# Hybrid mixer layer: scan branch rebuilt by chunks of four state tiles, its elementwise work and the gate sums from GpSimd to VectorE

## The chip, the cores and the metric

One core of a Trainium2 chip runs the whole program. The metric is the device time of one execution in microseconds (us). A run has several executions; of the kernel before three were timed, and one more was executed with the profiler.

## The reference, cut to what matters

Two layers, one after the other, on a sequence of 256 positions with 2048 features. A layer normalizes its input, projects it with one wide matrix, feeds four branches a to d of width 512 with slices of the projection, and sums them under gates:

```python
def _layer(x, ...):
    h = _rmsnorm(x, norm_g)
    proj = h @ w_in
    ya, yb, yc = ...                        # two attentions and a matrix recurrence
    yd = _branch_s5(d_u, ...) * silu(d_z)
    up = einsum('bsnw,nwd->bsnd', stack([ya, yb, yc, yd]), w_up)
    gates = sigmoid(gate + merge_b)
    merged = sum(gates * up, over the four branches)
    return x + merged @ w_out

def _branch_s5(u, ...):                     # 32 groups, 16 inputs and 64 complex states each
    bu_re, bu_im = einsum(u, bb_re), einsum(u, bb_im)
    x = scan over time of  x[t] = a * x[t-1] + bu[t]        # a complex
    y = einsum(x_re, c_re) - einsum(x_im, c_im) + d_skip * u
    y = gelu(y);  return y * sigmoid(y @ glu_w + glu_b)
```

The change concerns the branch d (`_branch_s5`) from the product with `bb` to the sum with `d_skip * u`, and the sum over the four branches.

## The kernel before, in words

**Weights and blocks.** Nearly all the work of TensorE is products of 128 positions (two halves t) with weight blocks of 512 columns. Weights come from HBM by SP's queue in units of 512 KB (tile `raw`, 1024 columns on 128 partitions). ScalarE rounds a unit to `wh` and VectorE computes `wl = raw - wh` (class `Stream`, line 355, `split`, line 369, three units ahead of their use). `block` (line 432) then makes three matmuls for each 128 rows and half: `wh*hH`, `wl*hH`, `wh*hL`. A projection block has 16 x 2 x 3 = 96 matmuls, an up block (a branch's output with `w_up`) 24. The two halves of a block go into two of four PSUM banks with the name `mm`, so a block can start once the block before the last has been evacuated.

**Order.** `layer_sequence` lists the blocks of a layer: first the projections for the branches, from the dilated attention on with gate blocks and up blocks in between, then the remaining gate and up blocks with `glu` behind the thirteenth gate, then the blocks with `w_out`. Work of the branches is written as generators (chains e, q, m, b, c, a, d; d is the scan branch). After each weight unit `tick` (line 411) steps these chains in the order `eqmbcad`, as long as a planner (class `Plan`, line 135) believes that VectorE, ScalarE and GpSimd are at most 2600 ns ahead of TensorE (`free`, line 202) and that what the step yielded as its needs is ready with two of four banks free (`can`, line 194). The planner holds a price for each instruction (class `Eng`, line 207) and assumes that VectorE and GpSimd shut each other out where they share a port (`port`, line 151). Each engine works through its instructions in the order in which they are issued. Since all go through one helper, every row has line 253, and instructions are told apart by their tiles.

**The scan branch** (`d_scan`, line 1207). The 2048 complex states lie in 16 tiles of 128, four to a chunk c. The rotation of the states is taken out by cosine and sine tables of a chunk (`d_table`, line 1143: its second step is eight instructions on VectorE, `dk` and `dr`, one pair for each tile), which leaves a real scan. For a tile: `enter` (line 1219) makes the input products (`dbu`, for two tiles together, 12 matmuls of 32 rows, each tile on its own row strip of the array), multiplies them by cosine and sine on VectorE (from PSUM into `dm`), and GpSimd adds and subtracts them. `scan` (line 1240) runs two `tensor_tensor_scan` on VectorE, then two products with cosine and sine on GpSimd (`dm`, `dn`). `leave` (line 1250) subtracts and adds on VectorE. The loop is a pipeline: step i enters tile i, scans tile i-1 and leaves tile i-2. After every second tile the output products (`dyp`) of two tiles follow, 32 output columns each on its own column strip, and one VectorE instruction per pair adds `d_skip * u` into `uT`. One step of the next chunk's table is taken behind each tile's scans, in the same step of the chain.

**The sum over branches** (`merge`, line 1379). Behind an up block VectorE multiplies its two PSUM banks by the gate, and for all but the first branch GpSimd adds the 1024 columns into the sum (`gate<-gate`, 12 per layer).

**Other users of GpSimd** that stay there: the small instructions of the reciprocal roots (`rsqrt`, line 461; for the attention's queries and keys in `a_evac`, line 694, whose PSUM banks are freed only by the product `aqk<-mm,ass` on VectorE behind the root), and the phases of the tables.

Of the kernel before, what the change touches and what calls it, by code (L numbers as in the profile page):

```python
# [12 lines left out]
ALU = mybir.AluOpType  # L13
AX = mybir.AxisListType

P = 128
S = 256
# [241 lines left out]
def hybrid_kernel(ctx: ExitStack, tc: tile.TileContext, x_in, pos, win, wup, wout, wuq, wukv, wglu, pp_in, db_in,  # L259
# [3 lines left out]
    V, A = Eng(plan, "DVE", nc.vector), Eng(plan, "ACT", nc.scalar)  # L263
    T, G = Eng(plan, "PE", nc.tensor), Eng(plan, "POOL", nc.gpsimd)
# [28 lines left out]
    def h2(shape, dt=F32, name="h2"):  # L293
        return hp.tile(shape, dt, tag="h2", name=name)
# [8 lines left out]
    def brps(name="br"):  # L303
        t = pbr.tile([P, 512], F32, tag="br", name=name)
        plan.bank(t)
        return t
# [171 lines left out]
    def bc(ap, shape):  # L478
        return ap.to_broadcast(shape)
# [663 lines left out]
    def d_table(o, c):  # L1143

        iota = c_("iota")
        r, k = s4([P, 4, S], name="dr"), s4([P, 4, S], name="dk")
        for j in range(4):
            i = 4 * c + j
            V.tensor_scalar(k[:, j], iota, o.dfull[:, i:i + 1], MAGIC, op0=ALU.mult, op1=ALU.add)
        V.tensor_scalar(k, k, MAGIC, None, op0=ALU.subtract)  # L1150
        yield
        for j in range(4):
            i = 4 * c + j
            V.scalar_tensor_tensor(k[:, j], iota, o.dhi[:, i:i + 1], k[:, j], op0=ALU.mult, op1=ALU.subtract)
            V.scalar_tensor_tensor(r[:, j], iota, o.dlo[:, i:i + 1], k[:, j], op0=ALU.mult, op1=ALU.add)
        yield
        cosT = s4([P, 4, S], name="cosT")
        yield from half_angle(r, r, cosT, k, cosT)
        o.tab[c] = (cosT, r)
        yield  # L1160
# [46 lines left out]
    def d_scan(o):  # L1207
        yield (o.du,)
        uT = s4([P, 4, S], name="uT")
        to_T(o.du, uT)  # L1210
        uH, uL = s4([P, 4, S], F32R, name="uH"), s4([P, 4, S], F32R, name="uL")
        A.copy(uH, uT)
        V.tensor_tensor(uL, uT, uH.bitcast(F32), op=ALU.subtract)
        o.tab = {}
        yield from d_table(o, 0)
        yield (uH, uL, o.bbH, o.bbL)
        xs, bu = {}, {}

        def enter(i):
            c, j = divmod(i, 4)  # L1220
            if i % 2 == 0:
                for i2 in (i, i + 1):
                    bu[i2] = brps("dbu").rearrange("p (r s) -> p r s", r=2)
                for r in range(2):
                    for i2 in (i, i + 1):
                        q = slice(32 * (i2 % 4), 32 * (i2 % 4) + 32)
                        for n, (w, u) in enumerate(((o.bbH, uH), (o.bbH, uL), (o.bbL, uH))):
                            T.matmul(bu[i2][:, r], lhsT=w[q, r, c], rhs=u[q, c], start=(n == 0), stop=(n == 2),
                                     tile_position=(32 * (i2 % 4), 0))
            ps = bu.pop(i)  # L1230
            cs = bc(o.tab[c][0][:, j][:, None, :], [P, 2, S])
            sn = bc(o.tab[c][1][:, j][:, None, :], [P, 2, S])
            m1, m2 = h2([P, 2, S], name="dm1"), h2([P, 2, S], name="dm2")
            V.tensor_tensor(m1, ps, cs, op=ALU.mult)
            V.tensor_tensor(m2, ps, sn, op=ALU.mult)
            G.tensor_tensor(m1[:, 0], m1[:, 0], m2[:, 1], op=ALU.add)
            G.tensor_tensor(m1[:, 1], m1[:, 1], m2[:, 0], op=ALU.subtract)
            xs[i] = (m1, m2, cs, sn)

        def scan(i):  # L1240
            m1, m2, cs, sn = xs[i]
            mg = bc(o.mag[:, i:i + 1], [P, S])
            for r in range(2):
                V.tensor_tensor_scan(m2[:, r], mg, m1[:, r], 0.0, op0=ALU.mult, op1=ALU.add)
            n2 = h2([P, 2, S], name="dn2")
            G.tensor_tensor(m1, m2, cs, op=ALU.mult)
            G.tensor_tensor(n2, m2, sn, op=ALU.mult)
            xs[i] = (m1, n2)

        def leave(i):  # L1250
            x, n2 = xs[i]
            V.tensor_tensor(x[:, 0], x[:, 0], n2[:, 1], op=ALU.subtract)
            V.tensor_tensor(x[:, 1], x[:, 1], n2[:, 0], op=ALU.add)
            xs[i] = x

        nxt = iter(())
        for i in range(19):
            if i < 16:
                c = i // 4
                if i % 4 == 0:  # L1260
                    if c:
                        for _ in nxt:
                            yield
                    nxt = d_table(o, c + 1) if c < 3 else iter(())
                enter(i)
                yield (xs[i - 1][0],) if i else ()
            if 0 <= i - 1 < 16:
                scan(i - 1)
                next(nxt, None)
                yield xs[i - 2] if i > 1 else ()  # L1270
            if i >= 2 and i - 2 < 16:
                leave(i - 2)
                c, j = divmod(i - 2, 4)
                if j % 2:
                    yield (xs[i - 3], xs[i - 2])
                    yp = brps("dyp")[:, :S]
                    for jj in (j - 1, j):
                        q = slice(32 * jj, 32 * jj + 32)
                        x = xs.pop(4 * c + jj)
                        for r in range(2):  # L1280
                            T.matmul(yp[q, :], lhsT=o.dc[:, r, 4 * c + jj], rhs=x[:, r], start=(r == 0), stop=(r == 1),
                                     tile_position=(0, 32 * jj))
                    q = slice(32 * (j - 1), 32 * (j + 1))
                    V.scalar_tensor_tensor(uT[q, c], uT[q, c], o.p("dskip")[q, c:c + 1], yp[q],
                                           op0=ALU.mult, op1=ALU.add)
                yield (uH, uL)
        o.dyT = uT

    def d_gelu(o):
# [55 lines left out]
    o = new_layer(0)  # L1345
# [4 lines left out]
    ps = brps("warm")  # L1350
# [3 lines left out]
    for d in range(4):  # L1354
        xb = s4([P, 2, 512], name="xb")
        if d == 0:
            for i in range(2):
                q = slice(256 * i, 256 * i + 256)
# [11 lines left out]
    for l in range(depth):  # L1370
# [8 lines left out]
        def merge(nm, ps):  # L1379
            d, n = int(nm[1]), int(nm[2])  # L1380
            gt = gate_t.pop(nm)
            first = n == UP_ORDER[0]
            if first:
                acc_t[d] = gt
            acc = acc_t[d]
            for t in range(2):
                V.scalar_tensor_tensor(gt[:, t], gt[:, t], 1.0, ps[t], op0=ALU.add, op1=ALU.mult)
            if not first:
                G.tensor_tensor(acc, acc, gt, op=ALU.add)
            if n == UP_ORDER[-1]:  # L1390
                spawn("m", merged(o, d, acc_t.pop(d)))

# [13 lines left out]
        for kind, nm in layer_sequence(l):  # L1406
            if kind == "in":
                if nm[0] == "g":
                    d, n = int(nm[1]), int(nm[2])
# [3 lines left out]
                ps = proj(nm)  # L1413
# [32 lines left out]
                else:  # L1446
                    gt = s4([P, 2, 512], name="gate")
# [172 lines left out]
```

## Time and profile before

| | us |
|---|---|
| median of 3 executions | 2090.07 |
| lowest, highest | 2087.39, 2090.59 |
| the profiled execution, its own time | 2088.86 |
| its span, first to last instruction | 2086.7 |
| TensorE busy | 2065.0 |
| VectorE busy | 1418.9 |
| ScalarE busy | 1034.8 |
| GpSimd busy | 446.9 |

The profile is one execution recorded by the hardware. PE is TensorE's matmuls, PEld its weight loads, DVE is VectorE, ACT ScalarE, POOL GpSimd. A busy time counts the time in which at least one instruction of the engine runs. Matmuls are pipelined and their ends are modelled, so that the time between two starts says more than a duration. Float32 matmuls of the branches appear as two records each. PEclk is the granted clock of TensorE as a share of 2.4 GHz.

### The profile page before, as it was taken

Reading aid. Unit: us, or ns where it says so; the run is one execution under the profiler, and the core shown is the slowest. Engines: PE = TensorE matmul, PEld = TensorE weight load, DVE = VectorE, ACT = ScalarE, POOL = GpSimd, SP = SyncE. Lnnn points to the kernel's source line nnn. Section 1 sums busy time; section 2 is a strip of 40 time slices with the busy share of each in tenths; the row PEclk is TensorE's granted clock in tenths of the full one; section 3 lists DMA queues with packets and bytes.
Section 4 is the critical chain, followed back from the end, with each engine's and each line's share of the span. In section 5 each row is a group of like instructions: output and inputs, shape, how many; then the busy total and the mean of one; then the engine's idle time right before and its main releaser. Section 6 shows DMA issues by size and latency. Waiting matters only on the chain.

```text
span 2086.7 us, 26821 instructions
## 1 busy us (share of the span) xinstructions
PE 2065.0 (99%) x9764; PEld 1702.1 (82%) x9764; DVE 1418.9 (68%) x1817; ACT 1034.8 (50%) x1574; POOL 446.9 (21%) x702
## 2 busy tenths in 40 slices
PE   9999999999999999999999999999999999999999
PEld 7888887788888888888888888887777888888887
DVE  5566578778777766667556765858777667667664
ACT  6656464454544544444456564455554445444442
POOL 2533114321242000001043121323223300001010
PEclk9999999999999999999999999999999999999999
DMA  7554354445555556656655543455445555556564
GB/s 266 182 187 166 123 176 167 156 163 170 183 191 173 183 199 206 204 202 208 232 188 182 192 162 124 175 166 191 163 167 187 185 178 183 205 204 205 197 212 171
DMA packets 111012, 384.60 MB, mean 184 GB/s; under 512 B 12321, under 2 KB 13217, under 8 KB 110881
## 3 DMA queue, kind: packets, MB, share of 16 engines
q1 hardware_dynamic: 108576, 378.40, 53.2%
q10 hardware_dynamic: 2304, 4.50, 0.6%
q8 instruction: 76, 1.25, 0.2%
q14 instruction: 56, 0.45, 0.1%
HBM read 378.66 MB, written 4.19 MB: 183 GB/s over the span
## 4 chain that ended last, share of the span: by engine, by line
PE 95%; DVE 3%; DMA 1%; POOL 1%; ACT 0%; issue 0%; SPq 0%; DVEq 0%; ACTq 0%
PE mm L253 86%; PE mb L253 2%; PE pv L253 1%; DVE dk L253 1%; PE tt L253 1%; PE dyp L253 1%; PE sc L253 1%; PE dbu L253 1%; DVE wl L253 1%; DVE dm L253 1%; DVE dr L253 1%; PE bsc L253 1%; PE pt L253 1%; DMA raw<-win 0%; PE xt L253 0%
## 5 line engine op out<-in xcount | busy, mean ns | idle before, releaser
L253 DVE TENSOR_TENSOR wl<-raw,wh 128x1024 fp32r<-128x1024 f32 (+1 forms) x694 | 909.0, 1323 | 533.8 <-ACT wh L253 530.8
L253 ACT CAST wh<-raw 128x1024 fp32r<-128x1024 f32 (+1 forms) x694 | 722.8, 1046 | 805.2 <-PE mm L253 690.7
L253 PE MATMUL mm<-wh,hH 128*128 128x512 f32 (+1 forms) x2240 | 877.0, 392 | 6.3 <-DVE gate L253 3.9
L253 PE MATMUL mm<-wl,hH 128*128 128x512 f32 (+1 forms) x2240 | 867.5, 387 | 2.6 <-DVE wl L253 2.6
L253 PE MATMUL mm<-wh,hL 128*128 128x512 f32 (+1 forms) x2240 | 866.7, 387 | 0.0
L253 PEld LDWEIGHTS mm<-wh,hH 128*128 128x128 f32 x2240 | 421.6, 188 | 97.5 <-issue 10.8
L253 PEld LDWEIGHTS mm<-wl,hH 128*128 128x128 f32 x2240 | 422.1, 188 | 88.0 <-DVE wl L253 5.5
L253 PEld LDWEIGHTS mm<-wh,hL 128*128 128x128 f32 x2240 | 421.6, 188 | 86.5 <-DVE hL L253 0.4
L253 POOL TENSOR_TENSOR gate<-gate 128x1024 f32<-128x1024 f32 x24 | 62.5, 2603 | 590.9 <-DVE gate L253 590.9
L253 POOL TENSOR_TENSOR dm<-dm,dm 128x256 f32<-128x256 f32 x64 | 76.3, 1213 | 354.9 <-DVE dm L253 345.9
L253 PE MATMUL mm<-wh,yH 128*128 128x512 f32 x256 | 101.3, 396 | 5.5 <-DVE aqk L253 5.5
L253 PE MATMUL mm<-wl,yH 128*128 128x512 f32 x256 | 100.6, 393 | 0.0
L253 PE MATMUL mm<-wh,yL 128*128 128x512 f32 x256 | 100.4, 392 | 0.0
L253 PE MATMUL mm<-wh,mH 128*128 128x512 f32 x256 | 100.2, 391 | 0.0
L253 PE MATMUL mm<-wh,mL 128*128 128x512 f32 x256 | 99.6, 389 | 0.0
L253 PE MATMUL mm<-wl,mH 128*128 128x512 f32 x256 | 99.6, 389 | 0.0
L253 POOL TENSOR_TENSOR dm<-dm,cosT 128x512 f32<-128x512 f32 x32 | 48.9, 1529 | 85.0 <-DVE dm L253 84.9
L253 PEld LDWEIGHTS mm<-wh,yH 128*128 128x128 f32 x256 | 48.7, 190 | 16.0 <-issue 5.9
L253 PEld LDWEIGHTS mm<-wh,yL 128*128 128x128 f32 x256 | 48.6, 190 | 10.2
L253 PEld LDWEIGHTS mm<-wl,yH 128*128 128x128 f32 x256 | 48.7, 190 | 9.8
L253 PEld LDWEIGHTS mm<-wh,mL 128*128 128x128 f32 x256 | 48.0, 188 | 9.9
L253 PEld LDWEIGHTS mm<-wh,mH 128*128 128x128 f32 x256 | 48.1, 188 | 9.8
(351 smaller groups left out, 1704.2 us busy)
## 6 DMA issues: line engine op xcount, KB each, us to landing
raw<-win SPq DMA_DIRECT2D x544, 512.0 KB, 3.7
raw<-wup SPq DMA_DIRECT2D x64, 512.0 KB, 4.2
raw<-wout SPq DMA_DIRECT2D x64, 512.0 KB, 4.2
mb<-mb_in SPq DMA_DIRECT2D x32, 256.0 KB, 4.4
xb<-x_in SPq DMA_DIRECT2D x7, 512.0 KB, 6.6
raw<-wuq SPq DMA_DIRECT2D x6, 512.0 KB, 4.1
raw<-win SPq DMA_DIRECT2D x8, 272.0 KB, 2.8
raw<-wglu SPq DMA_DIRECT2D x4, 512.0 KB, 4.4
```

Of the source, the lines that this page charges most:

```text
L253: return fn(*args, **kw)
```

## The change

The scan branch goes chunk by chunk. For a chunk the input products are made twice for two tiles, now alternating between the two row strips; each tile's four multiplications, two scans and all additions run on VectorE in three steps of the chain, the last of which also takes the step of the next table. The output products follow once for each chunk, for four tiles on four column strips, the real parts of all four first, and one instruction over 128 partitions adds `d_skip * u`. The sum over branches runs on VectorE. The core of the diff:

```diff
-            V.tensor_tensor(m1, ps, cs, op=ALU.mult)
-            V.tensor_tensor(m2, ps, sn, op=ALU.mult)
-            G.tensor_tensor(m1[:, 0], m1[:, 0], m2[:, 1], op=ALU.add)
-            G.tensor_tensor(m1[:, 1], m1[:, 1], m2[:, 0], op=ALU.subtract)
...
-            n2 = h2([P, 2, S], name="dn2")
-            G.tensor_tensor(m1, m2, cs, op=ALU.mult)
-            G.tensor_tensor(n2, m2, sn, op=ALU.mult)
...
-                    for jj in (j - 1, j):
-                        q = slice(32 * jj, 32 * jj + 32)
-                        x = xs.pop(4 * c + jj)
-                        for r in range(2):
-                            T.matmul(yp[q, :], lhsT=o.dc[:, r, 4 * c + jj], rhs=x[:, r], start=(r == 0), stop=(r == 1),
-                                     tile_position=(0, 32 * jj))
-                    q = slice(32 * (j - 1), 32 * (j + 1))
-                    V.scalar_tensor_tensor(uT[q, c], uT[q, c], o.p("dskip")[q, c:c + 1], yp[q],
-                                           op0=ALU.mult, op1=ALU.add)
...
+        for c in range(4):
+            for _ in nxt:
+                yield
+            nxt = d_table(o, c + 1) if c < 3 else iter(())
+            xs = []
+            for j0 in (0, 2):
+                yield (uH, uL, o.bbH, o.bbL)
+                bu = [brps("dbu").rearrange("p (r s) -> p r s", r=2) for _ in range(2)]
                 for r in range(2):
...
+                    for n, (w, u) in enumerate(((o.bbH, uH), (o.bbH, uL), (o.bbL, uH))):
+                        for e in range(2):
+                            q = slice(32 * (j0 + e), 32 * (j0 + e) + 32)
+                            T.matmul(bu[e][:, r], lhsT=w[q, r, c], rhs=u[q, c], start=(n == 0), stop=(n == 2),
+                                     tile_position=(32 * (j0 + e), 0))
+                yield (*bu,)
+                for e in range(2):
...
+                    V.tensor_tensor(m1, bu[e], cs, op=ALU.mult)
+                    V.tensor_tensor(m2, bu[e], sn, op=ALU.mult)
+                    V.tensor_tensor(m1[:, 0], m1[:, 0], m2[:, 1], op=ALU.add)
+                    V.tensor_tensor(m1[:, 1], m1[:, 1], m2[:, 0], op=ALU.subtract)
+                    yield
+                    mg = bc(o.mag[:, 4 * c + j:4 * c + j + 1], [P, S])
+                    for r in range(2):
+                        V.tensor_tensor_scan(m2[:, r], mg, m1[:, r], 0.0, op0=ALU.mult, op1=ALU.add)
+                    yield
+                    V.tensor_tensor(m1, m2, cs, op=ALU.mult)
+                    V.tensor_tensor(m2, m2, sn, op=ALU.mult)
+                    V.tensor_tensor(m1[:, 0], m1[:, 0], m2[:, 1], op=ALU.subtract)
+                    V.tensor_tensor(m1[:, 1], m1[:, 1], m2[:, 0], op=ALU.add)
+                    xs.append(m1)
+                    next(nxt, None)
+                    yield
+            yield (*xs,)
+            yp = brps("dyp")[:, :S]
             for r in range(2):
...
+                for j in range(4):
+                    T.matmul(yp[32 * j:32 * j + 32, :], lhsT=o.dc[:, r, 4 * c + j], rhs=xs[j][:, r], start=(r == 0),
+                             stop=(r == 1), tile_position=(0, 32 * j))
+            yield (yp,)
+            V.scalar_tensor_tensor(uT[:, c], uT[:, c], o.p("dskip")[:, c:c + 1], yp, op0=ALU.mult, op1=ALU.add)
...
             if not first:
-                G.tensor_tensor(acc, acc, gt, op=ALU.add)
+                V.tensor_tensor(acc, acc, gt, op=ALU.add)
```

## Rows read from the trace of the kernel before

**Rows 1.** Page, busy time of each engine.
```profile
PE 2065.0 (99%) x9764; PEld 1702.1 (82%) x9764; DVE 1418.9 (68%) x1817; ACT 1034.8 (50%) x1574; POOL 446.9 (21%) x702
```

**Rows 2.** Waits of PE: who waited for whom, us in total, times, longest.
```profile
PE mm L253 <- DVE aqk L253: 7.9, 2, 5.5
PE mm L253 <- DVE gate L253: 3.9, 1, 3.9
PE mm L253 <- DVE wl L253: 2.6, 4, 1.6
```

**Rows 3.** Chain of waits, 400 to 418 us: start, us, what.
```profile
410.32 0.39 DVE dk L253
410.74 0.48 DVE dr L253
...
412.15 1.42 DVE dk L253
...
413.59 1.36 DVE dr L253
...
416.93 0.69 DVE aqk L253
```

**Rows 4.** Stretches: length, busy PE, PEld, DVE, ACT, POOL (instructions), PEclk, DMA share, GB/s.
```profile
425.00:680.00 255.00, 255.00 (x1220) 206.74 (x1219) 195.51 (x251) 128.47 (x192) 76.03 (x74) 1.00 0.52 178
...
411.80:422.60 10.80, 5.27 (x14) 3.86 (x13) 8.79 (x11) 1.04 (x1) 2.87 (x2) 0.69 0.24 86
```

**Rows 5.** Timeline of PE, 417.5 to 420 us: start, us, instruction.
```profile
418.32 0.63 PE L253 MATMUL mm<-wl,yH 128*128 128x512 f32 x1
418.74 0.63 PE L253 MATMUL mm<-wh,yL 128*128 128x512 f32 x1
```

**Rows 6.** Timeline of PE, 376.6 to 378.6 us, around one group of output products.
```profile
376.67 0.39 PE L253 MATMUL mm<-wh,hL 128*128 128x512 f32 x1
376.99 1.06 PE L253 MATMUL dyp<-dm,dc 128*32 128x256 f32 x8
377.98 0.50 PE L253 MATMUL mm<-wh,hH 128*128 128x512 f32 x1
378.32 0.40 PE L253 MATMUL mm<-wl,hH 128*128 128x512 f32 x1
```

**Rows 7.** Timeline of PE, 434.4 to 437.4 us, output products followed by input products.
```profile
434.81 1.06 PE L253 MATMUL dyp<-dm,dc 128*32 128x256 f32 x8
435.80 0.39 PE L253 MATMUL dbu<-uH,bbH 32*128 32x256 f32 x2
```

**Rows 8.** Tile dyp: count, duration ns min/median/max, first and last start us.
```profile
L253 PE MATMUL dyp<-dm,dc x128: 379/379/404, 377.0 to 1661.3; 128*32 128x256 f32 x128
```

**Rows 9.** Groups of POOL, shapes apart: count, busy us, mean ns, idle before.
```profile
L253 POOL TENSOR_TENSOR dm<-dm,dm 128x256 f32<-128x256 f32 x64 | 76.3, 1213 | 354.9 <-DVE dm L253 345.9 <-PE mm L253 8.0 <-DVE rsi L253 0.9
L253 POOL TENSOR_TENSOR gate<-gate 128x1024 f32<-128x1024 f32 x24 | 62.5, 2603 | 590.9 <-DVE gate L253 590.9
L253 POOL TENSOR_TENSOR dn<-dm,dr 128x512 f32<-128x512 f32 x32 | 55.5, 1736 | 0.0
L253 POOL TENSOR_TENSOR dm<-dm,cosT 128x512 f32<-128x512 f32 x32 | 48.9, 1529 | 85.0 <-DVE dm L253 84.9
```

**Rows 10.** Tile dm on DVE: count, duration ns min/median/max, first and last start us.
```profile
L253 DVE TENSOR_TENSOR_SCAN dm<-mag,dm x64: 656/681/1228, 326.1 to 1645.2; 128x256 f32<-128x256 f32 x64
L253 DVE TENSOR_TENSOR dm<-dm,dn x64: 409/415/1511, 350.6 to 1651.4; 128x256 f32<-128x256 f32 x64
```

**Rows 11.** Timeline of DVE, 774 to 784 us, before and beside a gate sum of POOL.
```profile
776.18 1.23 DVE L253 TENSOR_TENSOR wl<-raw,wh 128x1024 fp32r<-128x1024 f32 x1 [1.54 <-ACT wh L253]
...
778.90 4.47 DVE L253 TENSOR_TENSOR wl<-raw,wh 128x1024 fp32r<-128x1024 f32 x2 [0.30 <-ACT wh L253]
```

**Rows 12.** Groups of DVE, shapes apart: count, busy us, mean ns, idle before.
```profile
L253 DVE TENSOR_TENSOR wl<-raw,wh 128x1024 fp32r<-128x1024 f32 x682 | 900.5, 1334 | 519.4 <-ACT wh L253 516.4
L253 DVE TENSOR_TENSOR_SCAN dm<-mag,dm 128x256 f32<-128x256 f32 x64 | 50.7, 832 | 0.0
```

More of the change, by code (lines that the diff above doesn't have):

```diff
@@ L1216, in d_scan @@
         yield (uH, uL, o.bbH, o.bbL)
[L1217 to L1223, printed above, removed]
-                for r in range(2):
[L1225 to L1233, printed above, removed]
-            V.tensor_tensor(m1, ps, cs, op=ALU.mult)
-            V.tensor_tensor(m2, ps, sn, op=ALU.mult)
-            G.tensor_tensor(m1[:, 0], m1[:, 0], m2[:, 1], op=ALU.add)
-            G.tensor_tensor(m1[:, 1], m1[:, 1], m2[:, 0], op=ALU.subtract)
-            xs[i] = (m1, m2, cs, sn)
@@ L1240, in scan @@
-        def scan(i):
-            m1, m2, cs, sn = xs[i]
-            mg = bc(o.mag[:, i:i + 1], [P, S])
-            for r in range(2):
-                V.tensor_tensor_scan(m2[:, r], mg, m1[:, r], 0.0, op0=ALU.mult, op1=ALU.add)
-            n2 = h2([P, 2, S], name="dn2")
-            G.tensor_tensor(m1, m2, cs, op=ALU.mult)
-            G.tensor_tensor(n2, m2, sn, op=ALU.mult)
[L1248 to L1276, printed above, removed]
-                    for jj in (j - 1, j):
-                        q = slice(32 * jj, 32 * jj + 32)
-                        x = xs.pop(4 * c + jj)
-                        for r in range(2):
-                            T.matmul(yp[q, :], lhsT=o.dc[:, r, 4 * c + jj], rhs=x[:, r], start=(r == 0), stop=(r == 1),
-                                     tile_position=(0, 32 * jj))
-                    q = slice(32 * (j - 1), 32 * (j + 1))
-                    V.scalar_tensor_tensor(uT[q, c], uT[q, c], o.p("dskip")[q, c:c + 1], yp[q],
-                                           op0=ALU.mult, op1=ALU.add)
-                yield (uH, uL)
@@ new lines, in d_scan @@
+        nxt = iter(())
+        for c in range(4):
[6 more added lines that the diff above has]
+                bu = [brps("dbu").rearrange("p (r s) -> p r s", r=2) for _ in range(2)]
+                for r in range(2):
+                    for n, (w, u) in enumerate(((o.bbH, uH), (o.bbH, uL), (o.bbL, uH))):
[5 more added lines that the diff above has]
+                for e in range(2):
+                    j = j0 + e
+                    cs = bc(o.tab[c][0][:, j][:, None, :], [P, 2, S])
+                    sn = bc(o.tab[c][1][:, j][:, None, :], [P, 2, S])
+                    m1, m2 = h2([P, 2, S], name="dm1"), h2([P, 2, S], name="dm2")
+                    V.tensor_tensor(m1, bu[e], cs, op=ALU.mult)
[16 more added lines that the diff above has]
+            yp = brps("dyp")[:, :S]
+            for r in range(2):
+                for j in range(4):
[3 more added lines that the diff above has]
+            V.scalar_tensor_tensor(uT[:, c], uT[:, c], o.p("dskip")[:, c:c + 1], yp, op0=ALU.mult, op1=ALU.add)
```

## The prediction

> **What bounds the kernel now.** I read the page's busy times first. TensorE (PE) shows 2065.0 us of a 2086.7 us span, 99%, and VectorE (DVE) 68% [rows 1]. So a microsecond is worth something only if PE issues less, or waits less. A busy PE also hides time, because matmul ends are modelled, so I then looked at three things: who PE waited for, what its clock did after each wait, and how far apart matmuls start.
>
> The waits of PE name three causes inside the part that the scan shares: 7.9 us for the projection's evacuation (aqk), 3.9 us for a gate's, 2.6 us for the low half of a weight (wl), 14.4 us together [rows 2]. They are a handful of events. The chain of waits through the longest shows what was in front: the block of eight table instructions of d_table. One of these takes 0.48 us when alone, and 1.42 and 1.36 us while a scan product of POOL (GpSimd) runs beside it; only after the block comes the evacuation that PE waits for [rows 3]. The stretch of and behind this stall has a mean granted clock of 0.69, so part of it ran at 1.2 GHz instead of 2.4, while the undisturbed stretch 425 to 680 has 1.00 [rows 4]. Behind the longest one matmuls start 0.43 us apart [rows 5] instead of 0.23. I count 27 such starts behind three stalls, 12 of them behind this one: 27 x 0.20 = 5.4 us. The stalls cost 14.4 + 5.4 = 19.8 us, and they all lie in the two scan windows (312 to 425 and 1230 to 1518).
>
> The last of PE's own time that the change touches is the output product dyp. One group costs: last matmul before it at 376.67, group at 376.99, next projection matmul at 377.98, the one after at 378.32 [rows 6]. Against a spacing of 0.23 that is 0.09 late going in, 0.99 inside, and 0.11 late coming out, which I take as 0.17 with the few that follow: 1.26 us. In six of the 16 groups a dbu group follows directly (434.81, then 435.80) and the way out is saved [rows 7], so those cost 1.08. All: 10 x 1.26 + 6 x 1.08 = 19.1 us. Its 128 recorded matmuls are 64 calls, each recorded as two matmuls of 256 columns [rows 8].
>
> **The change, part by part.**
>
> *Output products.* Before, a group is two tiles on two column strips: 8 matmuls in 0.99 us. As 8 x 0.20 us in a row they would take 1.6 us, so the two strips already run side by side, though the code writes one tile's products wholly ahead of the other's. Afterwards a group holds four tiles on four strips: 16 matmuls, half as many groups. If four strips overlap as two do, a group still lasts 1.26 us, and the sum is 8 x 1.26 = 10.1 us: **9.0 us gained**. If only two ever overlap, a group takes 8 x 0.21 + 0.16 + 0.26 = 2.1 us, sum 16.7, gain 2.4 us. The best end is 10 us (no way out is lost), the worst is nothing. I take 9, as the measured pair is the nearest row. The Trainium skill, "TensorE: Matmul & The Clock Gate", Part 3, gives three column strips a speed-up of 2.38, not 3. By that estimate the 0.83 us of strip time would be 1.05, and the gain 1.7 us smaller. No row here shows more than two strips.
>
> *Input products.* The dbu calls are reordered so that two row strips alternate. In the trace they alternate already: the first record of a dbu group holds both tiles' first product, 0.39 us for two [rows 7]. Number and groups stay. Nothing gained; the bounds are zero and one switch per group, 16 x 0.1 us either way.
>
> *Elementwise work from POOL to DVE.* POOL loses 64 additions of 256 columns, 32 + 32 products of 512, and 24 gate sums of 1024: 76.3 + 55.5 + 48.9 + 62.5 = 243 us of its 447 [rows 1, 9]. DVE gains the same instructions. A 256-column one on DVE has a median of 0.415 us [rows 10], a 1024-column one takes 1.23 [rows 11]; a 512-column one from SBUF I put halfway between by columns, 0.69. Sum: 64 x 0.415 + 64 x 0.69 + 24 x 1.23 = 100 us. Against it stands what POOL costs DVE now. Beside a gate sum of POOL (2.6 us on average, [rows 9]) two wl take 4.47 us, not 2 x 1.23 [rows 11], so each gate sum costs DVE 2 us and doing it there costs 1.23. All 682 wl average 1.334 [rows 12], which at 1.23 undisturbed is 682 x 0.104 = 71 us; the 64 scans average 0.832 [rows 12] with a minimum of 0.656 [rows 10], 11 us; the table instructions of [rows 3] come on top, about 1 us for each one caught. So 82 to 115 us go and 100 come. **DVE stays at about 1419 us**, bounds -15 and +20, and PE time does not follow directly.
>
> *What that does to the stalls.* The table block lasts 5.6 us in the longest stall (410.3 to 415.9, [rows 3]) and would last 8 x 0.46 = 3.7 us undisturbed: 1.9 us less. But the same generator step now runs two products and two additions on DVE (2 x 0.69 + 2 x 0.415, less 0.08 of overlap each, 1.9 us) ahead of the block, where two scans stood (2 x 0.66 less the same, 1.2 us): 0.7 us more. Net 1.2 us less for each of four stalls, 5 us. The two aqk stalls have a second cause: the reciprocal root behind aqk runs on POOL between the scan's products, and that queue is now free of them. I put 1 us on each. Shorter stalls leave the clock less time at its lower level; a third of 5.4 us is 1.8. **Together 8.5 us of 19.8.** The ends: all 19.8 gone, or, since every step falls in another place of the order, none gone and a few new ones.
>
> *What waits behind what.* No DMA is added, removed or moved; SP's queue is unchanged. On POOL the small root instructions now stand behind nothing large. On DVE the gate sum stands behind the two merges and in front of the next wl, which is issued three weight units ahead, 3 x 12 x 0.23 = 8.3 us; DVE is 68% busy over the span [rows 1], and in the gate stretch PE shows none of its waits; that covers 1.23 us. If the cover were gone each of the 24 would cost up to 1.2 us. The closing multiply-add is 8 instructions over 128 partitions instead of 16 over 64, on DVE, hidden in the same way. The scan branch's last product of the second layer is at 1661 [rows 8], and the glu block that needs its result comes behind the thirteenth gate, far later; a scan some tens of us later costs nothing by itself.
>
> *The sum.* 2088.9 (the profiled execution; its span is 2086.7) - 9.0 - 8.5 = **2071**. The median of the runs shown, 2090.07, is 1.2 us above that execution, so 2071 is if anything low by 1.
>
> **Rivals.**
> 1. *The stalls stay* (0.22). The eight table instructions are still one step, and the planner, which prices one at 396 ns by its formula (256 columns with a pointer) where the trace has 0.48 us [rows 3], still puts them ahead of an evacuation. Half the stalls are lost in one place and come back in another. Only the output products are won: 2088.9 - 9 = 2080.
> 2. *Four strips do not overlap* (0.10). Gain 2.4 instead of 9, stalls shorter all the same: 2088.9 - 2.4 - 8.5 = 2078. For it: no row shows four. Against it: two lose nothing [rows 6].
> 3. *The planner's new order is worse by about what the products win* (0.09): 2088 to 2091, no change.
> 4. *Slower: DVE becomes the bound in the scan* (0.07). All scan work is now in one in-order queue with wl. In the scan stretch 425 to 680 DVE is busy 195.5 of 255 us [rows 4]. If the stretching came from the small POOL instructions that stay, and not from those that go, the 71 us of scan work would land on top, 35 in each layer's 350 us or so of scan, and take it from 77% to 87%. It decides where the queue is over 8.3 us deep, the lead of wl. A step with a table block is 1.9 + 3.7 us and the planner lets DVE run 2.6 us ahead, 8.2 together, so just short of that point. If each of 32 tiles then cost its 1.9 us once in two, 30 us come: 2088.9 - 9 + 30 = 2110. Against it: the gate row shows the large POOL operation stretching wl by nearly its whole length.
>
> **How the numbers follow.** A difference of 0.2%, 4.2 us, is about what a measurement of this kernel can tell. The forecast has 0.52 with its own range 2058 (all stalls and 10 us of products gone) to 2077. With rivals 1 and 2 it is faster: 0.84. Rival 3 is the same: 0.09. Rival 4 is slower: 0.07. The range 2058 to 2086 holds the forecast and rivals 1 and 2; it leaves out rival 4 and most of rival 3, and a little below.
>
> **What would show it.** Right: dyp in 8 groups of 16 records, each about as long as a group of 8 before; wl's mean near 1.23; POOL near 200 us; DVE still near 1420; PE's waits for aqk, gate and wl under 10 us; PE clock 1.00 in all but one or two short stretches. Wrong: a dyp group of 2 us (rival 2); waits of PE as long as now with dk and dr in front (rival 1); wl late in many places of the scan, DVE over 90% there (rival 4).

## The result, and the profile after

The changed kernel has a median of 2061.66 us (four executions, 2060.98 to 2062.62) beside 2089.86 for the one before on the same chip: ratio 0.9867, 95% interval 0.9850 to 0.9885. That is 28 us gained; forecast were 19 against that median, and 17.9 against the profiled execution. The profiled execution of after took 2062.62 us with a span of 2060.5 us, so between the two profiles the span fell by 26.2 us. The same row of the page as [rows 1]:

```profile
PE 2050.3 (100%) x9764; PEld 1696.4 (82%) x9764; DVE 1397.8 (68%) x1961; ACT 1035.6 (50%) x1574; POOL 206.3 (10%) x550
```

PE issues as many matmuls as before. Its waits for the three tiles of [rows 2] (who waited for whom, us in total, times, longest):

```profile
PE mm L253 <- DVE wl L253: 1.1, 1, 1.1
...
PE mm L253 <- DVE gate L253: 0.5, 1, 0.5
```

The wait for aqk is gone, gate's fell from 3.9 to 0.5 and wl's from 2.6 to 1.1: 14.4 us have become 1.6. Only the wait for wl still has the old shape, the table block in front of what PE waits for. The chain of waits around it (start, us, what):

```profile
418.14 1.23 DVE wl L253
419.37 0.61 DVE dm L253
...
421.49 0.41 DVE dk L253
...
421.92 0.48 DVE dr L253
...
425.07 1.23 DVE wl L253
```

The block of eight runs from 421.49 to about 425.0, 3.5 us, and none of its instructions is stretched as those of [rows 3] were. With the four dm in front, two wl lie 6.9 us apart, and PE was 1.1 us short. That is the size of one step of the chain, seen from outside.

The output products, timeline of PE around one group (start, us, instruction), against [rows 6]:

```profile
380.52 0.39 PE L253 MATMUL mm<-wh,hL 128*128 128x512 f32 x1
380.83 1.07 PE L253 MATMUL dyp<-dm,dc 128*32 128x256 f32 x16
381.83 0.50 PE L253 MATMUL mm<-wh,hH 128*128 128x512 f32 x1
382.18 0.40 PE L253 MATMUL mm<-wl,hH 128*128 128x512 f32 x1
```

Sixteen records on four column strips take 1.00 us to the next projection matmul, where eight on two strips took 0.99. There are 8 such groups instead of 16. Counted with the ways in and out (what the start of the group and the first five starts behind it are late by), the groups took 18.9 us before and 9.8 after, 9.1 us less.

The groups of DVE, shapes apart (count, busy us, mean ns, idle before), against [rows 12]:

```profile
L253 DVE TENSOR_TENSOR wl<-raw,wh 128x1024 fp32r<-128x1024 f32 x682 | 826.7, 1223 | 529.4 <-ACT wh L253 526.2
L253 DVE TENSOR_TENSOR dm<-dm,dm 128x256 f32<-128x256 f32 x128 | 48.7, 421 | 2.2
L253 DVE TENSOR_TENSOR_SCAN dm<-mag,dm 128x256 f32<-128x256 f32 x64 | 40.6, 676 | 0.4
L253 DVE TENSOR_TENSOR gate<-gate 128x1024 f32<-128x1024 f32 x24 | 29.4, 1225 | 0.8
L253 DVE TENSOR_TENSOR dm<-dm,dr 128x512 f32<-128x512 f32 x32 | 22.2, 692 | 1.1
```

DVE took over 100 us of work and is busy 21 us less, because nothing large of POOL runs beside it any more: the mean wl fell from 1334 to 1223 ns, the mean scan from 832 to 676.

**Where the 26.2 us of span came from.** The 512-column matmuls start 0.227 us apart when nothing disturbs them. I added up, over the timeline of PE, what each such matmul's successor was late by, where it was more than 0.15 us. Before, that is 23.2 us: 14.1 in four stalls (1.8 at 345, 2.5 at 361, 5.7 at 412, 4.1 at 1510), 5.4 in the 27 starts at 0.43 us behind three of them, 3.7 in single late ones. After, it is 5.7. So 17.5 us came from late starts and 9.1 from the output products, 26.6 together, with 0.3 lost again on the input products: nothing else of size moved.

### The profile page after: what moved, and what is told of

Read it like the earlier page. It is cut to its first block, busy times and chain, and to the rows that moved or that the text cites. A ratio compares the mean times of both kernels' runs of the same rounds, so it can differ in the third digit from the quotient of the medians.

```text
span 2060.5 us, 26706 instructions
## 1 busy us (share of the span) xinstructions
PE 2050.3 (100%) x9764; PEld 1696.4 (82%) x9764; DVE 1397.8 (68%) x1961; ACT 1035.6 (50%) x1574; POOL 206.3 (10%) x550
## 4 chain that ended last, share of the span: by engine, by line
PE 95%; DVE 3%; DMA 1%; issue 0%; ACT 0%; SPq 0%; DVEq 0%; ACTq 0%
PE mm L253 87%; PE mb L253 2%; DVE dm L253 1%; PE pv L253 1%; PE tt L253 1%; DVE wl L253 1%; PE sc L253 1%; PE dbu L253 1%; PE bsc L253 1%; PE pt L253 0%; PE dyp L253 0%; PE cn L253 0%; PE xt L253 0%; DVE dk L253 0%; PE mt L253 0%
## 5 line engine op out<-in xcount | busy, mean ns | idle before, releaser
L253 DVE TENSOR_TENSOR wl<-raw,wh 128x1024 fp32r<-128x1024 f32 (+1 forms) x694 | 835.2, 1214 | 543.6 <-ACT wh L253 540.4
L253 PEld LDWEIGHTS mm<-wl,mH 128*128 128x128 f32 x256 | 48.1, 188 | 9.7
L253 DVE TENSOR_TENSOR dm<-dm,dm 128x256 f32<-128x256 f32 x128 | 48.7, 421 | 2.2
```

What stands on the lines that cost most here:

```text
L253: return fn(*args, **kw)
```

## The experiments

The theory after the result: the four strips are worth 9 us, and the stalls vanished because POOL's large operations no longer stretch DVE nor hold the chain back. The rivals: the order by chunks does it, or the length of the table's step, or the move of the gate sums.

**The output products alone.** After, with dyp in pairs again:

```diff
-            yield (*xs,)
...
+                yield (*xs[j0:],)
+                yp = brps("dyp")[:, :S]
+                for jj in (j0, j0 + 1):
+                    for r in range(2):
+                        T.matmul(yp[32 * jj:32 * jj + 32, :], lhsT=o.dc[:, r, 4 * c + jj], rhs=xs[jj][:, r],
+                                 start=(r == 0), stop=(r == 1), tile_position=(0, 32 * jj))
...
```

> The changed kernel with the output products in pairs of tiles again, each pair behind its own two tiles. Theory: 16 groups of 8 records of about 1.0 us, 8 to 9 us more on PE and nothing else: 2069 to 2072 us. Rival (four strips gain only on paper, the stalls moved instead): under 2066 us.

2071.63 us, ratio 0.9908 (0.9894 to 0.9923): 10.0 us above after. Its dyp groups take 19.5 us in all, 9.7 more than those of after, and PE waits for neither aqk, gate nor wl. (Between the two profiled executions it is 7.2 us of span, because the late starts of this run are 3.0 us against 5.7.) Fewer, wider groups are worth about what the products' sum said, and the stalls do not hang on them.

**The gate sums alone**, on DVE in the kernel before, and back on POOL in the kernel after:

```diff
-                G.tensor_tensor(acc, acc, gt, op=ALU.add)
+                V.tensor_tensor(acc, acc, gt, op=ALU.add)
```

> The kernel before with the gate sums alone on VectorE. Theory (the stalls come from GpSimd's scan work beside VectorE and ahead of the roots): VectorE loses the 50 us by which the 24 gate sums stretch wl and gains 24 x 1.23 = 30, so 20 us less busy, but no stall lies there: 2086 to 2092 us, PE's waits for aqk, gate and wl still over 10 us together. Rival (VectorE's total load sets the stalls): 5 us or more faster.

> The changed kernel with the gate sums back on GpSimd: wl's mean rises by some 50/682 = 0.07 us, VectorE busier by 20 us, no new wait of PE: 2060 to 2063 us. Rival (the gate sums on VectorE gave a part of the gain): 2066 us or more.

In before: 2089.26 us, ratio 0.9997 (0.9988 to 1.0006). In after: 2062.77, ratio 0.9870 (0.9856 to 0.9885). The first one's waits of PE:

```profile
PE mm L253 <- DVE aqk L253: 8.1, 2, 5.5
PE mm L253 <- DVE gate L253: 3.9, 1, 3.9
PE mm L253 <- DVE wl L253: 2.7, 4, 1.6
```

They are those of [rows 2]. DVE fell by 21 us (1418.9 to 1397.8) without a microsecond of time: where the gates run, DVE has room. With the sums back on POOL in after, wl is stretched again (1297 ns on average against 1223), and the time stays too.

**The scan's elementwise work alone.** The kernel before with its two additions and two products per tile on DVE; pipeline, pairs and gate sums as they were:

```diff
-            G.tensor_tensor(m1[:, 0], m1[:, 0], m2[:, 1], op=ALU.add)
-            G.tensor_tensor(m1[:, 1], m1[:, 1], m2[:, 0], op=ALU.subtract)
+            V.tensor_tensor(m1[:, 0], m1[:, 0], m2[:, 1], op=ALU.add)
+            V.tensor_tensor(m1[:, 1], m1[:, 1], m2[:, 0], op=ALU.subtract)
...
-            G.tensor_tensor(m1, m2, cs, op=ALU.mult)
-            G.tensor_tensor(n2, m2, sn, op=ALU.mult)
+            V.tensor_tensor(m1, m2, cs, op=ALU.mult)
+            V.tensor_tensor(n2, m2, sn, op=ALU.mult)
```

> The kernel before with the scan's additions and products on VectorE; pipeline over tiles, pairs of output products and gate sums on GpSimd stay. Theory (GpSimd's scan work makes the stalls): 2070 to 2076 us, PE's waits for aqk, gate and wl under 4 us, table instructions near 0.48 us each. Rival (the new structure by chunks makes the difference): 2085 to 2090 us, waits of 10 us and more.

2072.43 us, ratio 0.9913 (0.9899 to 0.9928). Of PE's waits in the shared part these are left:

```profile
PE mm L253 <- DVE wl L253: 1.4, 2, 0.9
...
PE mm L253 <- ACT wh L253: 1.2, 1, 1.2
```

17 us, nearly all that the stalls cost, from this move alone: late starts fell from 23.2 to 8.1 us. The mean wl is still 1297 ns, but the table's dk is back at 478 ns (681 before). So far the theory stands. Its other half is the same move undone in the kernel after:

```diff
-                    V.tensor_tensor(m1[:, 0], m1[:, 0], m2[:, 1], op=ALU.add)
-                    V.tensor_tensor(m1[:, 1], m1[:, 1], m2[:, 0], op=ALU.subtract)
+                    G.tensor_tensor(m1[:, 0], m1[:, 0], m2[:, 1], op=ALU.add)
+                    G.tensor_tensor(m1[:, 1], m1[:, 1], m2[:, 0], op=ALU.subtract)
...
-                    V.tensor_tensor(m1, m2, cs, op=ALU.mult)
-                    V.tensor_tensor(m2, m2, sn, op=ALU.mult)
+                    G.tensor_tensor(m1, m2, cs, op=ALU.mult)
+                    G.tensor_tensor(m2, m2, sn, op=ALU.mult)
```

> The changed kernel with the scan's additions and products back on GpSimd; chunks, four strips and gate sums on VectorE stay. Theory: the stalls return, 2072 to 2085 us, wl's mean at 1.27 us or more, PE's waits over 8 us. Rival (structure by chunks): 2060 to 2065 us, waits under 4 us.

2061.37 us, ratio 0.9861 (0.9845 to 0.9878): as fast as after, and the theory fell here. POOL is busy 381.4 us again, and yet of PE's waits for aqk, gate and wl only 0.6 us for wl is left. The groups of DVE say why:

```profile
L253 DVE TENSOR_TENSOR wl<-raw,wh 128x1024 fp32r<-128x1024 f32 x682 | 842.7, 1246 | 510.5 <-ACT wh L253 507.6
L253 DVE TENSOR_TENSOR_SCAN dm<-mag,dm 128x256 f32<-128x256 f32 x64 | 40.6, 675 | 21.5 <-POOL dm L253 21.5
...
L253 DVE TENSOR_TENSOR dm<-dm,dm 128x256 f32<-128x256 f32 x64 | 24.3, 420 | 54.6 <-POOL dm L253 54.6
```

The scan's mean is 675 ns, unstretched, and DVE idles 76 us waiting for POOL. Summed over DVE's instructions (what each takes above the short end, the 10th percentile, of its form while a POOL operation of over 0.9 us runs beside it) the stretching is 17 us, where the kernel before has 116. In the order by chunks one tile is worked through at a time: DVE waits for POOL's products, and the table's instructions come only behind the additions that waited. POOL has nothing large left by then. The pipeline of before did the opposite: it issued POOL's products for one tile and the table block right behind, so both ran side by side.

**The table beside POOL's products.** The kernel just described, with the table's step between products and additions, so that the two run side by side again:

```diff
                     G.tensor_tensor(m2, m2, sn, op=ALU.mult)
+                    next(nxt, None)
...
-                    next(nxt, None)
```

> As e4_scan_on_pool, but the table step stands between GpSimd's two products and VectorE's additions, so that its eight instructions run beside the products, as in the kernel before. Theory 2 (the stalls come from the table block running beside GpSimd's products, which the new order of a tile's steps ended): dk and dr average 0.6 us or more, PE's waits for aqk, gate and wl 5 us or more, 2066 to 2075 us. Rival (it is the pipeline over tiles as a whole, or the place of each step in the planner's order): 2060 to 2063 us, waits under 3 us.

2064.28 us, ratio 0.9876 (0.9862 to 0.9891), 2.9 us above the kernel it was made from: between the two ranges expected, and the intervals of the two ratios overlap. Its waits of PE, and its dr and dk on DVE:

```profile
PE mm L253 <- DVE aqk L253: 2.2, 1, 2.2
...
PE mm L253 <- DVE gate L253: 1.0, 1, 1.0
```

```profile
L253 DVE SCALAR_TENSOR_TENSOR dr<-cc,dlo,dk 128x256 f32<-128x256 f32 x32 | 20.1, 628 | 1.1
L253 DVE SCALAR_TENSOR_TENSOR dk<-cc,dhi,dk 128x256 f32<-128x256 f32 x32 | 19.5, 608 | 0.0
```

dk and dr have medians of 479 and 485 ns in the kernel after. Here they are stretched by more than a quarter, and waits for aqk and gate are back, 3.2 us in all where 5 or more were expected; late starts rise from 4.5 to 6.8 us. That has the sign of the mechanism, but at this strength it is worth 3 us of 17 at most, and this run alone does not show it.

**Contention with nobody waiting.** After, with two products and two sums of POOL per tile on scratch columns that nobody reads:

```diff
...
+                    for _ in range(2):
+                        G.tensor_tensor(scr, m2[:, :, 0:240], cs[:, :, 0:240], op=ALU.mult)
+                    for r in range(2):
+                        G.tensor_tensor(scr[:, r], m2[:, r, 0:240], m2[:, 1 - r, 0:240], op=ALU.add)
                     next(nxt, None)
```

> The changed kernel with as much GpSimd work as the scan had there before (two products and two sums for each tile, of 240 instead of 256 columns), on a scratch tile that nobody waits for, directly behind each tile's additions and so beside the table step. It is work beyond the reference. If the shared port alone makes the stalls: VectorE's wl mean over 1.27 us, VectorE 40 us or more busier, stalls back, 2070 to 2080 us. If a stretched VectorE is not enough (theory: there must also be someone waiting): wl stretched as well, but under 2066 us.

2087.70 us (2082.60 to 2089.46), ratio 0.9985 (0.9976 to 0.9995): 26 us above after, and above both ranges expected. That somebody must wait for POOL is refuted. The longest of PE's waits in its profile, one table group on DVE, and the timeline of DVE in front of one of these waits (PE starts again at 450.83, 2.1 us late):

```profile
PE mm L253 <- DVE wl L253: 15.5, 11, 2.9
```

```profile
L253 DVE SCALAR_TENSOR_TENSOR dk<-cc,dhi,dk 128x256 f32<-128x256 f32 x32 | 23.8, 745 | 0.0
```

```profile
442.42 1.80 DVE L253 TENSOR_TENSOR dm<-dm,dm 128x256 f32<-128x256 f32 x2
444.14 1.44 DVE L253 SCALAR_TENSOR_TENSOR dk<-cc,dhi,dk 128x256 f32<-128x256 f32 x1
...
449.16 0.48 DVE L253 SCALAR_TENSOR_TENSOR dr<-cc,dlo,dk 128x256 f32<-128x256 f32 x1
449.56 2.35 DVE L253 TENSOR_TENSOR wl<-raw,wh 128x1024 fp32r<-128x1024 f32 x2
```

Here the table step meets more of POOL's work, and nearly the whole gain of the change is lost. The profile has nine stalls of over 0.9 us behind the kernel's start, all for wl. In each a stretched step of the table stands in front of wl, directly in eight and with a gate's two instructions between in one: six times the block of eight, three times the first step of the table. By the Trainium skill, "SBUF — State Buffer", Who interferes with whom, the two engines lock each other out of a shared port; the trace agrees, 745 ns on average against 479.

**The block's length.** The kernel before with the eight table instructions in two steps of four:

```diff
             V.scalar_tensor_tensor(r[:, j], iota, o.dlo[:, i:i + 1], k[:, j], op0=ALU.mult, op1=ALU.add)
+            if j == 1:
+                yield
```

> The kernel before with the table block in two steps of four instructions. If the block's length ahead of an evacuation makes the stalls (the step named in the prediction): PE's waits for gate and wl together under 2 us and for aqk under 5 us, 2077 to 2084 us. Rival: the stalls move, waits of 10 us or more, 2085 to 2092 us.

2074.89 us, ratio 0.9927 (0.9912 to 0.9942), 14.4 us gained by one line, 2 us more than expected. Of the three causes one is left, and DVE is as stretched as ever:

```profile
PE mm L253 <- DVE aqk L253: 4.4, 3, 3.6
```

```profile
L253 DVE TENSOR_TENSOR wl<-raw,wh 128x1024 fp32r<-128x1024 f32 x682 | 891.2, 1320 | 501.0 <-ACT wh L253 498.1
...
L253 DVE SCALAR_TENSOR_TENSOR dk<-cc,dhi,dk 128x256 f32<-128x256 f32 x32 | 28.8, 899 | 0.0
```

wl has a mean of 1320 ns against 1334, dk 899 ns against 681. So the stretching alone does not make the stalls of before. That it makes them through the length of the step is not shown by this run, because here too the order moved: where the kernel before had its stalls at 345, 412 and 1510 us, no half of the block stands in front of the same matmul, and the longest of them went with an attention block whose evacuation began earlier (the table below).

**The reciprocal roots.** The prediction gave 1 us for each aqk stall to the roots on POOL. The kernel before with these on DVE:

```diff
-        rsqrt(ss)
+        rsqrt(ss, V)
```

> The kernel before with the reciprocal roots of the attention's queries and keys on VectorE instead of GpSimd. If the two aqk stalls come from the root standing behind the scan's work on GpSimd: aqk leaves PE's waits, 9 to 11 us faster, 2078 to 2081 us. If they come from the table block ahead of aqk on VectorE: aqk stays with 5 us or more, 2085 to 2092 us.

2079.56 us, ratio 0.9956 (0.9942 to 0.9970). Ten us faster, yet PE waits for aqk nearly as long as before, only in another place (at 1393 us instead of 412):

```profile
PE mm L253 <- DVE aqk L253: 6.7, 2, 6.3
...
PE mm L253 <- DVE gate L253: 2.4, 1, 2.4
```

The edit shifts the whole order, as that of the run before does, so the time of this run tells nothing certain of the roots.

**When aqk starts.** The traces do show when ScalarE begins the squares of an attention block and when DVE's aqk frees its banks. Before (first the two squares on ACT, then the two aqk on DVE; times are starts), and then after:

```profile
346.47 0.36 ACT L253 ACTIVATE aqk<-mm,r 128x128 f32<-128x128 f32 x1
...
396.79 0.36 ACT L253 ACTIVATE aqk<-mm,r 128x128 f32<-128x128 f32 x1
...
362.49 1.29 DVE L253 TENSOR_TENSOR aqk<-mm,ass 128x512 f32<-128x512 f32 x2 [0.68 <-POOL ass L253]
...
416.93 1.28 DVE L253 TENSOR_TENSOR aqk<-mm,ass 128x512 f32<-128x512 f32 x2
```

```profile
338.66 0.36 ACT L253 ACTIVATE aqk<-mm,r 128x128 f32<-128x128 f32 x1
...
386.77 0.36 ACT L253 ACTIVATE aqk<-mm,r 128x128 f32<-128x128 f32 x1
...
358.28 1.29 DVE L253 TENSOR_TENSOR aqk<-mm,ass 128x512 f32<-128x512 f32 x2 [1.32 <-POOL ass L253]
...
404.63 1.28 DVE L253 TENSOR_TENSOR aqk<-mm,ass 128x512 f32<-128x512 f32 x2
```

The two blocks ended on PE at 336.1 and 390.2 before, at 337.5 and 384.8 after. So the squares began 10.4 and 6.6 us behind the block before, 1.2 and 2.0 after; aqk was through 27.7 and 28.0 us behind it before, 22.1 and 21.1 after. PE wants the banks back when it has done one more block, 96 x 0.227 = 21.8 us plus the small products in between, 22 to 25 us. Both were late before, and after both are in time by no more than about 2 us. From the last square to aqk it takes 11.3 us on average over all 12 attention blocks before and 11.2 after: the roots are not faster, they start earlier. (Of these two blocks the first takes longer after, 16.7 us against 13.1, and the second less, 15.0 against 17.2.)

The same can be read in the other runs' traces. All times are us behind the end of the attention block on PE, for the first and the second block; block ends are read within about 0.2 us:

| kernel | squares begin | aqk is through | PE is done with one more block | PE starts late by |
|---|---|---|---|---|
| before | 10.4, 6.6 | 27.7, 28.0 | 24.7, 21.9 | 2.5, 5.7 |
| after | 1.2, 2.0 | 22.1, 21.1 | 22.3, 22.9 | none |
| scan's work on DVE, in before | 9.1, 3.7 | 23.8, 18.0 | 22.0, 21.6 | 1.4, none |
| scan's work on POOL, in after | 3.8, 1.0 | 17.1, 14.4 | 22.5, 22.5 | none |
| table beside POOL's products | 3.7, 1.0 | 24.4, 19.1 | 21.6, 22.9 | 2.3, none |
| roots on DVE, in before | 1.0, 9.2 | 21.9, 22.6 | 23.2, 21.6 | none, 0.5 |
| table step halved, in before | 6.4, 1.0 | 27.0, 21.1 | 22.8, 22.9 | 3.8, none |

In every row PE starts late just where aqk is through later than PE is done, by the difference less 0.4 to 0.6 us. So a deadline decides. (In the third row a wh of ACT ends at the same moment as aqk's first half, and the trace puts the wait down to that.) In the kernel before, the table block stands in front of aqk, with one wl between, in the second block only; in the first, DVE is idle for 0.68 us until the roots on POOL are done, as the line at 362.49 shows. What moves aqk against the deadline differs from run to run: earlier squares, a shorter way from the squares to aqk, or both. In the run with the halved step the 5.7 us stall went with squares that begin 1.0 us behind their block and not 6.6; the other block, with squares still at 6.4, keeps a stall, of 3.8 us.

**Does POOL's clock in the planner hold the squares back?** The kernel before, with POOL left out of the planner's limit:

```diff
-        return max(self.clk[e] for e in ("DVE", "ACT", "POOL")) <= lim
+        return max(self.clk[e] for e in ("DVE", "ACT")) <= lim
```

> The kernel before with one change to the planner: free() asks VectorE and ScalarE alone, not GpSimd. The instructions are the same, their order is not. Theory 3 (GpSimd's planned load holds all chains back, so that the squares behind the blocks aq1 and ak1 start 10.4 and 6.6 us late): the squares start within 2 to 5 us, aqk leaves PE's waits, 2076 to 2083 us. Rival (what stands on VectorE ahead of aqk decides, by the table block and the port): aqk still waited for, 5 us or more, 2086 to 2092 us.

2126.20 us, ratio 1.0175 (1.0158 to 1.0192), a miss: 2076 to 2083 was expected, or 2086 to 2092. The squares do start 3.0 and 1.2 us behind their blocks and aqk costs less, but new waits outweigh it, the two longest of them at 68 and 43 us, before the scan:

```profile
PE mm L253 <- ACT blat L253: 11.9, 1, 11.9
PE mm L253 <- DVE wl L253: 8.8, 7, 3.5
PE mm L253 <- ACT wh L253: 8.8, 2, 8.4
PE mm L253 <- DVE aqk L253: 3.5, 3, 2.0
```

Leaving that clock out brings the squares forward, and opens the queues to steps it had rightly held back. It does not show what brought them forward in the change.

**Towards a better version.** The table's step by itself in the kernel after:

```diff
                     xs.append(m1)
+                    yield
                     next(nxt, None)
```

> The changed kernel with the table step in a step of its own behind each tile. The waits left for wl and gate are 1.6 us and the two stalls 1.9: 2059 to 2061 us if they go; 2062 to 2065 if they only move.

2059.48 us, ratio 0.9853 (0.9839 to 0.9868), 2.2 us below after, with intervals that overlap; PE waits for wl, gate and aqk no more. Then the input products too on four strips, one group per chunk into four PSUM banks, evacuated in two steps, with the table's step by itself:

```diff
-            for j0 in (0, 2):
-                yield (uH, uL, o.bbH, o.bbL)
-                bu = [brps("dbu").rearrange("p (r s) -> p r s", r=2) for _ in range(2)]
...
+            bu = [brps("dbu").rearrange("p (r s) -> p r s", r=2) for _ in range(4)]
+            for r in range(2):
+                for n, (w, u) in enumerate(((o.bbH, uH), (o.bbH, uL), (o.bbL, uH))):
+                    for e in range(4):
+                        q = slice(32 * e, 32 * e + 32)
+                        T.matmul(bu[e][:, r], lhsT=w[q, r, c], rhs=u[q, c], start=(n == 0), stop=(n == 2),
+                                 tile_position=(32 * e, 0))
...
```

> The changed kernel with the input products of a whole chunk at once, four tiles on four row strips and four PSUM banks, evacuated in two steps, and the table step in a step of its own. If four row strips overlap as two do: 8 dbu groups of 24 records of about 0.9 us, 9 us less on PE, and no new waits: 2051 to 2055 us. Rival (the longer VectorE step of 3.7 us behind the group, or the held banks, make PE wait): 2058 to 2070 us.

**2054.44 us**, ratio 0.9828 (0.9813 to 0.9843): 7.2 us below after, 5.0 below the run with the table's step by itself, the fastest of all. First a group of after, then one of this kernel, timelines of PE:

```profile
1556.01 0.39 PE L253 MATMUL dbu<-uH,bbH 32*128 32x256 f32 x2
...
1556.70 0.28 PE L253 MATMUL dbu<-uH,bbL 32*128 32x256 f32 x2
1556.91 0.50 PE L253 MATMUL mm<-wh,hH 128*128 128x512 f32 x1
```

```profile
1522.84 0.39 PE L253 MATMUL dbu<-uH,bbH 32*128 32x256 f32 x4
...
1523.53 0.28 PE L253 MATMUL dbu<-uH,bbL 32*128 32x256 f32 x4
1523.74 0.50 PE L253 MATMUL mm<-wh,hH 128*128 128x512 f32 x1
```

From the first dbu to the next projection matmul it is 0.90 us in both, for 12 records and for 24. In all, the dbu groups fall from 17.8 us in after to 9.8, counted as the dyp groups above. Not all of these 8 us arrive: the late starts of this run are 4.4 us, against 2.5 in the run with the table's step by itself.

## Why the prediction was right, and where it was off

The time, 2061.66, lies in the range but near its low end, 2058, which the prediction had put at all stalls gone; one of its two gains was right, the other half of what it was.

**The output products** (9.0 forecast): 9.1 between the profiles, 10.0 by the run with pairs. The step held in each part: 8 groups, each as long as one of two strips, with the same ways in and out. (A dbu group follows directly in five of the 16 groups before, not six as the sum has it: 0.2 us.) Rival 2 is refuted. By the Trainium skill, "TensorE: Matmul & The Clock Gate", Part 3, three column strips give 2.38 and not 3; here four strips lose nothing against two (1.00 us against 0.99), and the measurement decides.

**The input products** (nothing): 17.5 us before, 17.8 after. Held.

**Elementwise work on DVE** (stays near 1419, -15 to +20): 1397.8, six below the range's lower end. The prices added were right (421 ns for the taken 415, 692 for 690, 1225 for 1230, 100 us in all). What went was at the upper bound of 82 to 115: summed over all DVE instructions as above, the stretching was 116 us before and is under 2 after. PE gained nothing by this 21 us as such, as the runs with the gate sums show.

**The stalls** (8.5 of 19.8 forecast; 17.5 measured, of the 23.2 us of late starts): this is the step that failed, "together 8.5 us of 19.8". Its term "net 1.2 us less for each of four stalls" priced the table's step correctly (3.5 us where 3.7 was reckoned, behind four elementwise instructions of DVE), but put the block in front of all four stalls, where the trace has it in front of three, and treated a stall as a sum that shrinks by what its block shrinks. It is an overrun of a deadline, as the table of blocks shows: once the second aqk is through 21 us behind its block and not 28, nothing is left of a stall of 5.7 us, and of the slow clock behind it. The clock's 5.4 us, the starts at 0.43 us behind the stalls of the scan, went with these (the granted clock of 312 to 425 us is 0.95 before and 1.00 after), where the step credited a third. And the 1 us for roots "on POOL between the scan's products" is not borne out as a shorter way: on average the way from the squares to aqk is as long as before, and what moved is its beginning.

What makes the stalls can be read across the runs. Those with next to none of the old ones (after, gate sums back, pairs, both moves of the scan's work, both better versions) have the table's dk at 478 or 479 ns on average, though wl is stretched to 1297 ns in two of them. The others, with dk from 608 to 899 ns, all have stalls. So it is the table step beside POOL's large operations that counts, not the stretching of wl. The scratch work, which put this back into the kernel after, cost 26 us. How this step reaches PE is shown there, where it stands in front of wl, and in the kernel before for the stalls at 345, 412 and 1510 us, where it stands in front of a wl, an aqk and a gate. That it also delays the squares, and by them the aqk at 361, is not shown, since the order of the steps moved in every run.

Two parts of the change each take most of the stalls away: POOL out of the scan (17 us, in the kernel before), and the order by chunks even with POOL in the scan (as fast as after). In the change itself the move of the elementwise work is therefore not needed for the time. In the kernel before, it took the stalls away by itself. The halved table step took 14 us away too, with the table's instructions stretched more than before and the order changed.

**The waits that might have come** (rival 4, DVE the bound): none. In the stretch 425 to 680 of [rows 4] the row of after is

```profile
425.00:680.00 255.00, 253.42 (x1236) 207.80 (x1235) 198.22 (x306) 130.63 (x202) 12.59 (x31) 1.00 0.54 181
```

DVE is busy 198.2 of 255 us, 78% against 77%, far from the 87% of the rival. Rival 1 foresaw the wl wait of the chain above, but as half of the stalls; it is one of 1.1 us.

**Open.** Why the squares begin 9 and 5 us earlier in the new order was not settled. The planner's clocks are the candidate, and the run that took one of them away moved the squares, but moved too much else to decide. Nor is the length of the table's step parted from its place in the order: the run that halved it changed both.

## What to carry to other kernels

Where PE runs at 99% and waits in a handful of places, find each wait's deadline and the longest unbroken step in the evacuating engine's queue ahead of it: a change that brings the evacuation in before its deadline takes the whole stall away, not only the part by which the step shrinks. Where a planner orders the steps, an edit of one step moves the others, so look in the trace which of them now stands in front of the wait. Here, moving work between engines that stretch each other paid only where the stretched instructions stood in front of such a deadline. Small matmuls on 32 rows or 32 columns should fill all four strips of the array in one group, since the group lasts as long as with two.

## What the runs showed of the hardware

Four strips overlap as fully as two, for columns (16 records in 1.00 us, 8 in 0.99) and for rows (24 in 0.90, 12 in 0.90). The order in which the code writes the strips' matmuls did not matter: the alternated dbu groups of after take 0.91 us each (median), as those of before, which are written tile after tile. And what stretches DVE here is POOL's large operations: the 550 instructions left after, nearly all small, keep POOL busy for 206 us and stretch DVE by about 2 us in all.
